# Thirty-two tokens of a 384-token dense stage move to a gathering stage that packs four slots into a step

## The chip, the core and the metric

One core of a Trainium2 chip runs the whole program. The metric is the device time of one execution in microseconds, and the time of a kernel is the median of several executions. The core has five engines that run side by side, each in its own program order: TensorE (PE, with its weight loads as PEld), VectorE (DVE), ScalarE (ACT), GpSimd (POOL) and SyncE (SP). SP does nothing but issue DMAs; ACT and POOL issue some too. Semaphores order one engine behind another.

## The reference, cut to what matters

The reference is two layers of an encoder trunk on 512 tokens (two sequences of 256) of width 1024. Each layer has a token mixer and a PEER channel mixer. Only PEER is touched:

```python
q = (ht @ wq).reshape(T, 8, 256)                       # 8 heads
s1, s2 = q[..., :128] @ k1.T, q[..., 128:] @ k2.T      # 128 keys each
v1, i1 = top_k(s1, 16); v2, i2 = top_k(s2, 16)
vs, ic = top_k(v1[..., :, None] + v2[..., None, :], 16)    # of 256 pairs
idx = i1[ic // 16] * 128 + i2[ic % 16]                 # an expert of 16384
g = softmax(vs)
a = einsum('td,thkd->thk', x, u_tab[idx])              # 8*16 = 128 slots a token
y = einsum('thk,thkd->td', g * gelu(a), v_tab[idx])
```

So every token picks 128 of 16384 experts; an expert is one row of 1024 in `u_tab` and one in `v_tab`.

## The kernel before, in words

All 512 tokens lie in columns, channels in partitions. `hH` and `hL` hold the normed input as a high and a low part in fp32r, and each product with a weight is made of three matmuls (`mm3`, L181 to L184): high weight by low data, high by high, low weight by high data. Weights come two chunks of 128 at a time as one 1 MB load (`wraw`, L133), are cast to the high part by ACT (`wh`, L120), and DVE (in the stages u and v) or POOL (elsewhere) subtracts to get the low part (`wl`, L121). Two buffers of each exist.

PEER of a layer runs in this order. **Queries** (`queries`, L737): 16 products of 512 columns, then scores against the keys (L744) and, on DVE, the sixteen largest of each (`top16`, L730). Early in it `row_copy` (L411) turns the last 128 tokens by PE and ACT into `hrow`, one token to a partition. **Routing** (`route`, L778) finds experts and weights of 128 tokens at a time on DVE.

Then the tokens go two ways. The first 384 (`TD`) are **dense**. Stage u (the loop over c, 128 chunks) multiplies all of `u_tab` by them: 24 matmuls of 384 columns a chunk, then GELU on ACT (L1011, L1017), and most results go to HBM (`a_d`). Between these, `gates` (L862) builds the tokens' gate matrices from one-hots: for four tokens two DVE instructions (L894, L898) and eight small matmuls (L872), and ACT's copy goes to HBM (`g_d`). Stage v (the loop over n, 128 chunks) reads both back (`va`, `vg`), multiplies them (`wf`, L995), splits (`sH`, `sL`) and multiplies with all of `v_tab`, again 24 matmuls of 384 columns a chunk, summed in eight PSUM banks.

The last 128 tokens are **gathered** (`gathered`, L911), token to partition. Step j of 128 fetches the 128 rows of `u_tab` that slot j of each token names (an indirect DMA of 128 rows by 4 KB issued by POOL, L926, four buffers, three ahead) and DVE multiplies and sums them with `hrow` (L937). After that 128 steps fetch rows of `v_tab`, and DVE adds each, weighted, to `yrow` (L945). At the end PE turns `yrow` back (L1082), and `residual` (L541) adds all of it to x.

The order on each engine is written out by hand. In stage u, `gathered` advances by at most 1.1 steps a chunk for 64 chunks, then so that `GU` steps are done by chunk 127; `gates` advances at 0.9 four-token steps a chunk until chunk 64 and then evenly until chunk 101; `route_tiles` (L839) routes the three dense tiles of 128 meanwhile. In stage v the rest of the steps are spread over 124 chunks. `tc.issue_after(st["last"])` puts these instructions behind the latest weight subtraction on DVE.

```python
while done - 1 < (GS * (c - c0) if c < CM else
                  GS * (CM - c0) + (GU - GS * (CM - c0)) * (c - CM) / (127 - CM)):
```

`norm` (L383) writes `hH`, `hL`, and with L404 a copy `hq` of the last 128 tokens.

## Time and profile before

| what | value |
|---|---|
| median of 3 runs | 3411.75 us (3403.14 to 3413.47) |
| the profiled execution's own time | 3406.75 us |
| its span, first to last instruction | 3404.9 us |
| mean granted TensorE clock | 0.978 |
| stage u of layer 0 | 618.9 to 1212 us |
| stage v of layer 0 with the residual | 1212 to 1750 us |
| stage v of layer 1 with the residual | 2863.4 to 3401 us |

A row of a profile names line, engine, operation and tiles as out<-in. Busy time of PE is the time in which at least one matmul is under way; since matmuls overlap, the distance between starts tells its pace. The DMA share is the time that packets took, over 16 engines and the stretch; it goes over 1 where packets of two queues overlap. A wait is named by who waited and for whom.

### The profile page before, as it was taken

Reading aid. Unit: us, or ns where it says so; the run is one execution under the profiler, and the core shown is the slowest. Engines: PE = TensorE matmul, PEld = TensorE weight load, DVE = VectorE, ACT = ScalarE, POOL = GpSimd, SP = SyncE. Lnnn points to the kernel's source line nnn. Section 1 sums busy time; section 2 is a strip of 40 time slices with the busy share of each in tenths; the row PEclk is TensorE's granted clock in tenths of the full one; section 3 lists DMA queues with packets and bytes.
Section 4 is the critical chain, followed back from the end, with each engine's and each line's share of the span. In section 5 each row is a group of like instructions: output and inputs, shape, how many; then the busy total and the mean of one; then the engine's idle time right before and its main releaser. Section 6 shows DMA issues by size and latency. Waiting matters only on the chain.

```text
span 3404.9 us, 47985 instructions
## 1 busy us (share of the span) xinstructions
PE 3274.4 (96%) x18758; PEld 3034.7 (89%) x18758; DVE 2714.8 (80%) x4689; ACT 1346.2 (40%) x1631; POOL 1106.9 (33%) x682
## 2 busy tenths in 40 slices
PE   7999979999999999999989998899999999999999
PEld 3778758999999999999978886689999999999999
DVE  6797997998898567777766589899979866777776
ACT  3443223345566333333335432334546543333232
POOL 4322453143232322333333234314423233223331
PEclk9999989999999999999989998899999999999999
DMA  6332552389899989999932236317999997899996
GB/s 244 123 137 88 197 193 88 138 313 351 314 349 344 317 287 321 348 339 356 341 131 86 87 137 214 119 72 278 340 335 331 345 340 280 302 351 335 348 334 238
DMA packets 271414, 867.46 MB, mean 255 GB/s; under 512 B 20241, under 2 KB 119633, under 8 KB 222801
## 3 DMA queue, kind: packets, MB, share of 16 engines
q1 hardware_dynamic: 174418, 500.49, 41.9%
q0 software_dynamic: 73728, 268.47, 22.0%
q10 hardware_dynamic: 23040, 95.43, 7.2%
q8 instruction: 147, 2.41, 0.3%
q14 instruction: 81, 0.66, 0.1%
HBM read 764.17 MB, written 97.52 MB: 253 GB/s over the span
## 4 chain that ended last, share of the span: by engine, by line
PE 72%; DVE 16%; DMA 7%; issue 3%; ACT 1%; POOL 1%; SPq 0%; DVEq 0%; ACTq 0%; POOLq 0%
PE y L182 9%; PE y L184 9%; PE y L183 9%; PE a L182 9%; PE a L184 9%; PE a L183 9%; DVE junk L259 5%; DMA wraw<-w_st 3%; PE G L872 3%; PE zin L182 2%; PE zin L183 2%; PE zin L184 2%; DMA mraw<-w_modT 2%; DVE wl L121 1%; PE q L182 1%
## 5 line engine op out<-in xcount | busy, mean ns | idle before, releaser
L120 ACT CAST wh<-wraw 128x2048 fp32r<-128x2048 f32 (+1 forms) x380 | 610.0, 1611 | 1185.8 <-PE y L183 354.2
L121 DVE TENSOR_TENSOR wl<-wraw,wh 128x2048 fp32r<-128x2048 f32 x248 | 568.3, 2291 | 371.3 <-ACT wh L120 371.0
L182 PE MATMUL a<-hL,wh 128*128 128x384 f32 x2048 | 698.8, 341 | 0.4 <-ACT wh L120 0.2
L184 PE MATMUL a<-hH,wl 128*128 128x384 f32 x2048 | 688.5, 336 | 10.9 <-DVE wl L121 10.9
L182 PE MATMUL y<-sL,wh 128*128 128x384 f32 x2048 | 686.2, 335 | 2.0 <-DVE sL L121 1.9
L183 PE MATMUL a<-hH,wh 128*128 128x384 f32 x2048 | 686.8, 335 | 0.0
L184 PE MATMUL y<-sH,wl 128*128 128x384 f32 x2048 | 684.5, 334 | 0.0
L183 PE MATMUL y<-sH,wh 128*128 128x384 f32 x2048 | 684.4, 334 | 0.0
L926 POOL DMA_INDIRECT row<-u_rows,idx x256 | 359.0, 1402 | 806.7 <-DVE row L937 563.8
L926 POOL DMA_INDIRECT row<-v_rows,idx x256 | 338.0, 1320 | 733.1 <-DVE yrow L945 698.5
L121 POOL TENSOR_TENSOR wl<-wraw,wh 128x1024 fp32r<-128x1024 f32 x132 | 359.3, 2741 | 645.3 <-ACT wh L120 645.3
L184 PEld LDWEIGHTS a<-hH,wl 128*128 128x128 f32 x2048 | 385.7, 188 | 14.0 <-DVE wl L121 14.0
L182 PEld LDWEIGHTS y<-sL,wh 128*128 128x128 f32 x2048 | 384.5, 188 | 4.2 <-DVE sL L121 3.7
L182 PEld LDWEIGHTS a<-hL,wh 128*128 128x128 f32 x2048 | 385.7, 188 | 1.0 <-ACT wh L120 1.0
L183 PEld LDWEIGHTS a<-hH,wh 128*128 128x128 f32 x2048 | 385.9, 188 | 0.0
L183 PEld LDWEIGHTS y<-sH,wh 128*128 128x128 f32 x2048 | 384.6, 188 | 0.0
L184 PEld LDWEIGHTS y<-sH,wl 128*128 128x128 f32 x2048 | 384.5, 188 | 0.0
L945 DVE SCALAR_TENSOR_TENSOR yrow<-row,ga,yrow 128x1024 f32<-128x1024 f32 x254 | 325.3, 1281 | 0.2
L259 DVE SCALAR_TENSOR_TENSOR junk<-mraw,cb 128x1024 bf16<-128x1024 f32 x176 | 304.6, 1731 | 21.4 <-DMA mraw<-w_modT 17.7
L937 DVE SCALAR_TENSOR_TENSOR row<-row,hrow 128x1024 f32<-128x1024 f32 x256 | 308.7, 1222 | 4.5 <-DMA row<-u_rows,idx 4.5
L182 PE MATMUL zin<-hL,wh 128*128 128x512 f32 x544 | 219.8, 404 | 4.9 <-DVE hL L406 4.8
L184 PE MATMUL zin<-hH,wl 128*128 128x512 f32 x544 | 215.5, 396 | 1.7 <-POOL wl L121 1.7
(255 smaller groups left out, 4616.7 us busy)
## 6 DMA issues: line engine op xcount, KB each, us to landing
wraw<-w_st SPq DMA_DIRECT2D x314, 1024.0 KB
g_d<-stg ACTq DMA_DIRECT2D x48, 1024.0 KB
vg<-g_d SPq DMA_DIRECT2D x32, 1536.0 KB
mraw<-w_modT SPq DMA_DIRECT2D x88, 512.0 KB
a_d<-a ACTq DMA_DIRECT2D x104, 384.0 KB
va<-a_d SPq DMA_DIRECT2D x52, 768.0 KB
pre<-w_st SPq DMA_DIRECT2D x8, 1024.0 KB
wsh<-w_mod SPq DMA_DIRECT2D x8, 512.0 KB
```

What stands on the lines that cost most here:

```text
L120: nc.scalar.copy(h, src)
L121: return (engine or nc.vector).tensor_sub(lo, src, h.bitcast(F32))
L182: nc.tensor.matmul(out, lhsT=a[0], rhs=b[1], start=first, stop=False)
L183: nc.tensor.matmul(out, lhsT=a[0], rhs=b[0], start=False, stop=False)
L184: st["pe"] = nc.tensor.matmul(out, lhsT=a[1], rhs=b[0], start=False, stop=last).ins
L259: st["mod"] = nc.vector.scalar_tensor_tensor(junk, w, 1.0, cb[:, s, :], op0=OP.mult, op1=OP.mult, accum_out=modc[l][:, j, s:s + 1]).ins
L872: nc.tensor.matmul(p[:, k, :], lhsT=oh[:, k // 2, 1, :, k % 2], rhs=o1[:, k // 2, n, :, k % 2], start=n == 0, stop=n == 1)
L926: nc.gpsimd.indirect_dma_start(out=r[:, :], out_offset=None, in_=tab[:, :], in_offset=bass.IndirectOffsetOnAxis(ap=idx[:, j:j + 1], axis=0))
L937: nc.vector.scalar_tensor_tensor(r, r, 1.0, hrow, op0=OP.mult, op1=OP.mult, accum_out=a[:, j:j + 1])
L945: nc.vector.scalar_tensor_tensor(yrow, r, a[:, j:j + 1], yrow, op0=OP.mult, op1=OP.add)
```

## The change

`TD` falls from 384 to 352: the dense stages and `gates` handle 32 tokens less. Those tokens, numbers 352 to 383, join the gathering. 32 more steps for each table serve them: the 128 partitions of a step hold 32 tokens four times, and partition group g takes the slots 32g to 32g+31, so a token's 128 slots are done in 32 steps. Their routing is still made with the third tile; four DMAs on SP's queue copy it into `egx` in that layout. `hqx` is a copy of these tokens in the norm, POOL repeats it four times along the columns, and PE and ACT turn it into a second `hrow`. The second `yrow` holds four partial sums per token, and one fp32 matmul per 128 channels with a 0/1 matrix `fold_x` adds them up at the end. It takes over the buffer of `hq`. `GU` rises from 132 to 178, out of 320 steps (`STEPS`) in place of 256.

```diff
...
@@ -34,13 +34,16 @@
 T = 512
 TS = 256
 NT = 4
-TD = 384
+NX = 32
+XG = 128 // NX
+TD = 384 - NX
 ND = TD // 16
 VG = 8
 NC = 64
 CAND = ((0, 0, 1, 16), (16, 1, 4, 8), (40, 4, 8, 4), (56, 8, 16, 1))
 GSCALE = 32768.0
-GU = 132
+GU = 178
+STEPS = 256 + 2 * NX
 R0 = 104
 GEND = 101
 PRE = 4
...
@@ -401,19 +404,29 @@
                 for c, B, A in half:
                     st["act"] = nc.scalar.activation(hH[:, k, c], t1[:, c], AF.Identity, bias=B).ins
                 if hq is not None:
-                    nc.scalar.activation(hq[:, k, :], t1[:, TD:], AF.Identity, bias=half[1][1])
+                    nc.scalar.activation(hq[:, k, :], t1[:, 384:], AF.Identity, bias=half[1][1])
+                    nc.scalar.activation(hqx[:, k, :], t1[:, TD:384], AF.Identity, bias=half[1][1])
                 for c, B, A in half:
                     st["dve"] = nc.vector.scalar_tensor_tensor(hL[:, k, c], t1[:, c], B, hH[:, k, c].bitcast(F32),
                                                                op0=OP.add, op1=OP.subtract).ins
                 filler = pull(filler, 2)
             run_all(filler or [])
 
-    def row_copy(hrow, hq):
-        for q in range(2):
-            p = bank([128, 4, 128], "hn")
-            for k in range(4):
-                nc.tensor.transpose(p[:, k, :], hq[:, 4 * q + k, :], ident)
-            nc.scalar.copy(hrow[:, q * 512:(q + 1) * 512], p.rearrange("p a b -> p (a b)"))
+    def row_copy(pool_, hrows, hq, hqx):
+
+        for i, hrow in enumerate(hrows):
+            for q in range(2):
+                p = bank([128, 4, 128], "hn")
+                for k in range(0, 4, 2):
+                    src = hq[:, 4 * q + k:4 * q + k + 2]
+                    if i:
+                        h = hqx[:, 4 * q + k:4 * q + k + 2]
+                        src = pool_.tile([128, 2, 128], F32, name="hx")
+                        nc.gpsimd.tensor_copy(src.rearrange("p k (g t) -> p k g t", t=NX),
+                                              h[:, :, None].to_broadcast([128, 2, XG, NX]))
+                    for c in range(2):
+                        nc.tensor.transpose(p[:, k + c, :], src[:, c, :], ident)
+                nc.scalar.copy(hrow[:, q * 512:(q + 1) * 512], p.rearrange("p a b -> p (a b)"))
 
 
     def mixer(l, fx):
...
@@ -836,12 +849,17 @@
         nc.vector.tensor_mul(eg[:, 2], eg[:, 2], z[:, :, None].to_broadcast([128, H, TOPK]))
         yield 1.0
 
-    def route_tiles(l, rp, pools, iotak, val, ixu, tiles):
-        for t in range(TD // 128):
+    def route_tiles(l, rp, pools, iotak, val, ixu, tiles, egx):
+        for t in range(3):
             while len(tiles) > 1:
                 yield 1.0
             eg = rp.tile([128, 3, NH, TOPK], F32, name="eg", bufs=1)
             yield from route(rp, iotak, val, ixu, t, eg)
+            if t == 2:
+                ef = eg.rearrange("p j h k -> p j (h k)")
+                for g in range(XG):
+                    nc.sync.dma_start(egx[g * NX:(g + 1) * NX], ef[128 - NX:, :, g * NX:(g + 1) * NX])
+                st["egx"] = l
             for _ in range(EGD):
                 yield 10.0
             p = bank([128, 3, 128], "egT")
@@ -879,12 +897,12 @@
             if g == 3:
                 nc.scalar.dma_start(g_d[l][t * 8 + b], stg.pop(b))
 
-        for tt in range(TD // 128):
+        for tt in range(3):
             while not tiles:
                 yield 1
             t, E16, g16 = tiles[0]
             rp = pools[0]
-            for b in range(8):
+            for b in range(min(8, ND - 8 * t)):
                 for g in range(4):
                     t0 = b * 16 + g * 4
                     oh = rp.tile([128, 2, 2, 128, 2], F16, name="o12", bufs=LAG + 2)
@@ -908,20 +926,29 @@
                 yield 1
             tiles.pop(0)
 
-    def gathered(l, gp, rp, iotak, val, ixu, eg, hrow, yrow):
+    def gathered(l, gp, rp, iotak, val, ixu, eg, egx, hrows, yrows):
+
+
         yield from route(rp, iotak, val, ixu, NT - 1, eg, HS, NH)
         yield ROUTED
         ef = eg.rearrange("p j h k -> p j (h k)")
-        idx = gp.tile([128, 128], U32, name="idx")
-        nc.vector.tensor_scalar(ef[:, 0], ef[:, 0], 128.0, float(l * 16384), op0=OP.mult, op1=OP.add)
-        nc.vector.tensor_add(idx, ef[:, 0], ef[:, 1])
-        a = gp.tile([128, 128], F32, name="ga")
+        idx = gp.tile([128, 128 + NX], U32, name="idx")
+        a = gp.tile([128, 128 + NX], F32, name="ga")
+
+        def index(e, c):
+            nc.vector.tensor_scalar(e[:, 0], e[:, 0], 128.0, float(l * 16384), op0=OP.mult, op1=OP.add)
+            nc.vector.tensor_add(idx[:, c], e[:, 0], e[:, 1])
+
+        index(ef, slice(0, 128))
         rows = {}
-        seq = [(tab, j) for tab in (u_rows, v_rows) for j in range(128)]
+        seq = [(tab, j) for tab in (u_rows, v_rows) for j in range(128 + NX)]
         AHEAD = 3
 
         def fetch(i):
             tab, j = seq[i]
+            if tab is u_rows and j == 128:
+                assert st["egx"] == l
+                index(egx, slice(128, 128 + NX))
             r = gp.tile([128, D], F32, name="row", bufs=AHEAD + 1)
             nc.gpsimd.indirect_dma_start(out=r[:, :], out_offset=None, in_=tab[:, :],
                                          in_offset=bass.IndirectOffsetOnAxis(ap=idx[:, j:j + 1], axis=0))
@@ -933,22 +960,25 @@
             if i + AHEAD < len(seq):
                 fetch(i + AHEAD)
             r = rows.pop(i)
-            if i < 128:
+            hrow, yrow, n = (hrows[1], yrows[1], NX) if j >= 128 else (hrows[0], yrows[0], 32)
+            if tab is u_rows:
                 nc.vector.scalar_tensor_tensor(r, r, 1.0, hrow, op0=OP.mult, op1=OP.mult, accum_out=a[:, j:j + 1])
-                if j % 32 == 31:
-                    c = slice(j - 31, j + 1)
+                if j % n == n - 1:
+                    c = slice(j - n + 1, j + 1)
                     nc.scalar.activation(a[:, c], a[:, c], AF.Gelu)
-                    nc.vector.tensor_mul(a[:, c], a[:, c], ef[:, 2, c])
-            elif j == 0:
-                nc.vector.tensor_scalar(yrow, r, a[:, 0:1], None, op0=OP.mult)
+                    w = egx[:, 2, :] if j >= 128 else ef[:, 2, c]
+                    nc.vector.tensor_mul(a[:, c], a[:, c], w)
+            elif j % 128 == 0:
+                nc.vector.tensor_scalar(yrow, r, a[:, j:j + 1], None, op0=OP.mult)
             else:
                 nc.vector.scalar_tensor_tensor(yrow, r, a[:, j:j + 1], yrow, op0=OP.mult, op1=OP.add)
             yield 1.15
 
-    def peer(l, hrow, hq):
+    def peer(l, hrows, hq, hqx):
         with ExitStack() as px:
             gp = px.enter_context(pool(name=f"gp{l}", bufs=1))
-            yrow = gp.tile([128, D], F32, name="yrow")
+            yrows = [gp.tile([128, D], F32, name="yrow"), hq.rearrange("p k n -> p (k n)")]
+            egx = gp.tile([128, 3, NX], F32, name="egx")
             iotak = gp.tile([128, TOPK, TOPK], F16, name="iotak")
             iota = gp.tile([128, 128], F32, name="iota")
             nc.sync.dma_start(iota, c_iota)
@@ -962,14 +992,14 @@
             prx = ExitStack()
             rb = prx.enter_context(pool(name=f"pr{l}", bufs=1, side=RIGHT))
             eg = gp.tile([128, 3, NH, TOPK], F32, name="egl")
-            queries(l, val, ixu, hrow, hq, rb, route(rp, iotak, val, ixu, NT - 1, eg, 0, HS))
+            queries(l, val, ixu, hrows, hq, hqx, rb, route(rp, iotak, val, ixu, NT - 1, eg, 0, HS))
             vx = ExitStack()
             vp = None
             gx = ExitStack()
             pools = []
-            ga = gathered(l, gp, rp, iotak, val, ixu, eg, hrow, yrow)
+            ga = gathered(l, gp, rp, iotak, val, ixu, eg, egx, hrows, yrows)
             tiles = []
-            rt = route_tiles(l, rp, pools, iotak, val, ixu, tiles)
+            rt = route_tiles(l, rp, pools, iotak, val, ixu, tiles, egx)
             gt = gates(l, pools, iota2, tiles)
             res = {}
             ablk, gblk = {}, {}
@@ -1031,7 +1061,7 @@
                             gq = 1
                         g0 = SG * (min(c + 1, CG) - c1)
                         with tc.issue_after(st["last"]) if B2 else ExitStack():
-                          while gt is not None and gq - 1 < g0 + (104 - g0) * max(0, c + 1 - CG) / (GEND - CG):
+                          while gt is not None and gq - 1 < g0 + (4 * ND + 8 - g0) * max(0, c + 1 - CG) / (GEND - CG):
                             gt = pull(gt, 1)
                             gq += 1
                     with tc.issue_after(st["last"]):
@@ -1070,7 +1100,7 @@
                             ds_ = slice(d * 128, (d + 1) * 128)
                             mm3(y[d][:, :TD], (w[0][:, ds_], w[1][:, ds_]), s, n == 0, False)
                     with tc.issue_after(st["last"]):
-                        while done - 1 < min(256, GU + (256 - GU) * (n + 1) / 124):
+                        while done - 1 < min(STEPS, GU + (STEPS - GU) * (n + 1) / 124):
                             next(ga)
                             done += 1
                     if n == 126:
@@ -1079,7 +1109,8 @@
                     ds_ = slice(d * 128, (d + 1) * 128)
                     for w, s, last in tail:
                         mm3(y[d][:, :TD], (w[0][:, ds_], w[1][:, ds_]), s, False, last)
-                    nc.tensor.transpose(y[d][:, TD:], yrow[:, ds_], ident)
+                    nc.tensor.transpose(y[d][:, 384:], yrows[0][:, ds_], ident)
+                    nc.tensor.matmul(y[d][:, TD:384], lhsT=yrows[1][:, ds_], rhs=fold_x, start=True, stop=True)
                     residual(l, 40, d, y[d], 0, T)
 
 
...
```

The part left out adds `fold_x` to the constants, and hands the new tiles through `queries` and `peer`.

## Rows read from the trace of the kernel before

**Rows 1.** The page's first part: busy time, share of the span and instructions of each engine.
```profile
PE 3274.4 (96%) x18758; PEld 3034.7 (89%) x18758; DVE 2714.8 (80%) x4689; ACT 1346.2 (40%) x1631; POOL 1106.9 (33%) x682
```
**Rows 2.** The chain that ended last, from 618 to 1750 us, by line.
```profile
by line: PE y L184 15.5%; PE y L182 15.5%; PE y L183 15.5%; PE a L182 13.7%; PE a L184 13.5%; PE a L183 13.4%; PE G L872 4.0%; DMA wraw<-w_st 1.5%; DVE wl L121 1.4%; DMA row<-u_rows,idx 1.1%; POOL acc L359 0.7%; issue 0.5%; DVE scr L732 0.4
```
**Rows 3.** The timeline of PE: start, duration; 256 columns, then 384, 18 intervals each.
```profile
253.79 0.28 PE L182 MATMUL iv<-idft,y 128*128 128x256 f32 x1
...
255.94 0.28 PE L182 MATMUL iv<-idft,y 128*128 128x256 f32 x1
...
2999.82 0.33 PE L183 MATMUL y<-sH,wh 128*128 128x384 f32 x1
...
3002.94 0.33 PE L183 MATMUL y<-sH,wh 128*128 128x384 f32 x1
```
**Rows 4.** Stretches: length, each engine's busy us, PEclk, DMA share, GB/s.
```profile
533.00:618.00 85.00, 83.60 (x427) 71.12 (x425) 77.63 (x487) 31.75 (x48) 27.30 (x12) 1.00 0.25 88
618.90:769.00 150.10, 146.49 (x887) 143.28 (x885) 147.03 (x451) 68.82 (x80) 55.14 (x34) 0.99 0.70 249
769.00:916.00 147.00, 147.00 (x973) 143.19 (x971) 121.49 (x226) 72.64 (x81) 45.66 (x36) 1.00 0.92 333
916.00:1076.00 160.00, 160.00 (x1185) 155.08 (x1184) 146.06 (x206) 99.16 (x106) 45.24 (x34) 1.00 0.93 345
1076.00:1212.00 136.00, 134.05 (x818) 132.63 (x816) 82.48 (x93) 52.94 (x59) 43.64 (x33) 1.00 0.88 313
1212.00:1750.00 538.00, 533.85 (x3082) 533.32 (x3081) 406.14 (x326) 174.09 (x137) 167.44 (x129) 1.00 0.92 322
1500.00:1520.00 20.00, 20.00 (x118) 20.00 (x117) 14.73 (x13) 5.42 (x5) 5.10 (x5) 1.00 1.07 375
2863.40:3401.00 537.60, 535.28 (x3081) 532.98 (x3080) 405.51 (x325) 166.93 (x126) 159.24 (x121) 1.00 0.90 318
```
**Rows 5.** DVE's groups, 916 to 1076 us: count, busy us, mean ns, idle before.
```profile
L937 DVE SCALAR_TENSOR_TENSOR row<-row,hrow 128x1024 f32<-128x1024 f32 x35 | 42.6, 1223 | 0.0
L121 DVE TENSOR_TENSOR wl<-wraw,wh 128x2048 fp32r<-128x2048 f32 x17 | 38.9, 2290 | 3.0 <-ACT wh L120 3.0
L898 DVE TENSOR_TENSOR o<-o,g 128x1024 f16<-128x1024 f16 x51 | 34.6, 692 | 11.0 <-PE G L872 11.0
L894 DVE TENSOR_TENSOR o<-E,iota 128x1024 f16<-128x1024 f16 x51 | 33.6, 690 | 0.0
```
**Rows 6.** DVE's groups, 1212 to 1750 us.
```profile
L945 DVE SCALAR_TENSOR_TENSOR yrow<-row,ga,yrow 128x1024 f32<-128x1024 f32 x124 | 158.8, 1281 | 0.0
L121 DVE TENSOR_TENSOR wl<-wraw,wh 128x2048 fp32r<-128x2048 f32 x63 | 144.4, 2292 | 123.3 <-ACT wh L120 123.2
```
**Rows 7.** DMA view, 1212 to 1750 us: rate in 40 slices, packets, two issue lines.
```profile
GB/s 239 333 288 280 354 237 342 356 289 371 315 333 401 303 371 294 357 392 315 370 307 357 401 286 369 323 344 399 309 372 316 360 370 318 378 302 328 213 163 111
DMA packets 73961, 173.04 MB, mean 322 GB/s; under 512 B 3648, under 2 KB 46656, under 8 KB 65856
...
vg<-g_d SPq DMA_DIRECT2D x14, 1536.0 KB
va<-a_d SPq DMA_DIRECT2D x24, 768.0 KB
```
**Rows 8.** DMA view, 916 to 1076 us: rate in 40 slices, packets.
```profile
GB/s 415 258 225 326 390 374 360 374 122 276 406 374 268 426 414 373 421 395 287 410 369 372 338 306 327 316 347 312 249 416 428 375 378 365 328 356 322 329 344 334
DMA packets 11571, 55.21 MB, mean 345 GB/s; under 512 B 1292, under 2 KB 1292, under 8 KB 7846
```
**Rows 9.** The tile row, whole span: the gathers on POOL, and their landing.
```profile
L926 POOL DMA_INDIRECT row<-v_rows,idx x256: 933/1408/3616, 1184.4 to 3367.1; - x128
...
DMA to landing us min/median/max: 4.9/8.1/10.4
```
**Rows 10.** The timeline around the row copy of layer 0: start, duration.
```profile
531.74 4.73 POOL L121 TENSOR_TENSOR wl<-wraw,wh 128x1024 fp32r<-128x1024 f32 x2 [33.42 <-ACT wh L120]
...
532.16 1.04 PE L415 MATMUL hn<-mats,hq 128*128 128x128 f32 x8
...
533.62 0.49 DVE L731 MAX8 val<-sc 128x8 f32<-128x128 f32 x2 [14.59 <-ACT sc L747]
```
**Rows 11.** ACT's groups, 500 to 519 us (the norm ahead of PEER).
```profile
L404 ACT ACTIVATE hq<-t,modc 128x128 f32<-128x128 f32 x8 | 3.1, 391 | 0.0
```
**Rows 12.** PE's groups, 3390 to 3403 us (the end of layer 1).
```profile
L1082 PE MATMUL y<-mats,yrow 128*128 128x128 f32 x8 | 2.2, 271 | 0.0
```

19 lines of the change are left out of this document (10 added, 9 removed).

## The prediction

> **What bounds the kernel now.** I read the page first: PE is busy for 96% of the span and DVE for 80% [rows 1], so PE leads, but an average hides the stages. The chain that ended last tells where. From 618 to 1750 us, stages u and v of layer 0, the matmuls of u and v hold 87% of it and the gate matmuls 4% [rows 2]. So the matmuls' own pace sets these stages, and the next view must give it: with 384 columns 18 starts take 3.12 us, 173.3 ns each, with 256 columns 2.15 us, 119.4 ns each [rows 3]. That is 0.421 ns a column. The stretches show what stands next in line [rows 4]. Stage u falls into four of about 32 chunks each. DVE is busy for 147.0 of 150.1 us in the first, 121.5 of 147 in the second, 146.1 of 160 in the third, 82.5 of 136 in the fourth. In stage v it has 406 of 538 us. The DMA share is 0.88 to 0.93 everywhere after the first stretch. Two other resources are thus near their limits, and a shorter matmul pays only where neither is reached first.
>
> **The shorter matmuls.** At 352 columns the line between the two paces gives 173.3 - 32 x 0.421 = 159.8 ns, 13.5 ns less. A stage has 128 x 24 = 3072 such matmuls, so PE's need falls by 41.4 us in each of the four stages (166 us in all), or 10.4 us in a quarter of stage u. The weight loads do not hold the pace, because 119 ns was reached with one for every matmul [rows 3].
>
> **The gathering's extra work in stage u.** Up to chunk 64 nothing moves: 1.1 steps a chunk. Behind it come 46 more steps than before (178 for 132) over 63 chunks, 23.4 in each of the last two quarters. Each costs DVE 1.22 us [rows 5] and the DMA engines 128 rows of 4 KB, 0.524 MB. Eight of 96 gate steps fall away; some seven of them lie in the third quarter, each with 0.69 + 0.69 us of DVE [rows 5] and 1.05 MB / 4 of stores.
>
> First quarter: DVE is already busy for 147.0 of 150.1 us and its work is unchanged. PE can gain 3 us at most; I take 1. Second quarter: PE 147.0 - 10.4 = 136.6, DVE 121.5, so all 10 us arrive. Third quarter: DVE needs 146.1 + 23.4 x 1.22 - 7 x 1.38 = 165 us, PE at most 150, and the bytes become 55.2 [rows 8] + 12.3 - 2.3 = 65.2 MB. Slices of 4 us reached 428 GB/s there, the mean was 345 [rows 8]: 152 to 189 us. I take 400 GB/s, since slices of 13 us in stage v reached 401 [rows 7] and 20 us held 375 [rows 4]; that makes 163 us, under DVE's 165. With a little for the two meeting: 167, a loss of 7. Fourth quarter: DVE 82.5 + 28.5 = 111, PE 134 - 10.4 = 124, bytes 0.313 x 136 = 42.6 + 12.3 - 0.7 = 54.2 MB, at 400 GB/s 136 us. PE's gain is lost to the transfers; with some unevenness 139, a loss of 3. **Stage u: 1 + 10 - 7 - 3, a gain of 1 us** out of 593 (between 21, rival a, and -21, rival b).
>
> **Stage v.** 142 steps for 124, so 18 more at 1.28 us [rows 6] or 23 us of DVE, which then has at most 429 us of work for 497, and covers it: the time in which it waited for ACT's cast before a weight subtraction, 123 us [rows 6], takes the new steps. Bytes: 173.0 + 9.4 - 3.4 (a twelfth of 14 vg and 24 va loads) = 179.0 MB [rows 7]. PE alone would end the stage after 538 - 41 = 497 us. By rate over share, 322 / 0.92 = 350 GB/s, the transfers take 511 us; at 375 GB/s [rows 4] 477. I take 503: **a gain of 35 us a layer** (25 to 41). What is late next is a weight load or a row behind another queue's packets.
>
> **Smaller parts, per layer.** Row copy: PE must turn the repeated tokens, and its transposes stand in program order behind four POOL copies through one buffer. The nearest row is POOL's subtraction of 1024 columns, 4.73 / 2 = 2.4 us [rows 10]; a quarter of that is 0.6, two transposes are 0.26 (1.04 / 8 each [rows 10]), four rounds 3.4 us. POOL is also busy until 536.5 with two subtractions, while PE would be there at 533.2: 3.3 us more. Behind the waiting transposes stand the scores, and DVE waits for those. But DVE has just started its first scores at 533.6 [rows 10] and is the fuller engine behind (77.6 of 85 us, then 147 of 150 [rows 4]), so PE's 7 us come back in part; I take 3 (0 to 8). Two more ACT copies lie beside it. Norm: eight ACT instructions, each under the 391 ns of four times the columns [rows 11], 0 to 3 us; taken 0.5, because PE still has the queries to do. SP's queue: four DMAs, 49 KB together, wait there for DVE's routing of the third tile, with weight loads behind; but those wait for later DVE work in any case, so nothing, and if DVE ran behind by a routing instruction about 1 us. POOL's further 64 gathers at 1.4 us [rows 9] lie in its idle time. Fold: eight fp32 matmuls of 32 columns in the closing chain, each under the 271 ns of the transposes there [rows 12]: taken 1.5 us (0 to 2.2). **Together 5 us lost** (1 to 13).
>
> **Sum.** 1 + 35 - 5 = 31 us a layer, 62 us in two. The profiled execution took 3406.75 us (span 3404.9 and 1.85 around it), so 3344.75. It is 5.0 us under the median of the three runs, 3411.75; on that median the forecast is **3350 us**, or -1.8%.
>
> **The rivals.**
> (a) PE stays the bound almost everywhere: DVE's surplus in the third quarter is taken up by its idle time in the second and fourth. For it: DVE has 54 us idle in the fourth. Against it: instructions are issued in a fixed order, so idle time cannot be borrowed back. With the third quarter level and the fourth 10 us shorter stage u gains 21, v 41, the small parts take 3: 59 a layer, 3411.75 - 118 = 3294.
> (b) The DMA engines have no more to give than rate over share tells: 345 / 0.93 = 371 GB/s in the third quarter makes 176 us (+16), 313 / 0.88 = 356 in the fourth 152 us (+16), and v takes 511 (-27). With -1 and -10 of the first quarters and 5 of the small parts that is -1 a layer, 3410. For it: shares of 0.9. Against it: the share counts packets twice where two queues overlap, and 1.07 at 375 GB/s is such a stretch [rows 4]. The Trainium skill, in "DMA: Bandwidth & Descriptors", section "Where 436 GB/s comes from", says that the memory side binds transfers from HBM at about 358 GB/s for a core; by that the third quarter would take 182 us, the fourth 151, stage v 500, and the whole about 3400. The trace does not agree with it as a ceiling: 401 GB/s stood over 13 us [rows 7].
> (c) Slower: the loop of four row buffers binds. A buffer is free again after landing (8.1 us median, 10.4 at most [rows 9]) and one DVE step of 1.22 us. The fourth quarter asks for 57 steps in 136 us, 2.39 us each, which the loop gives up to a landing of 4 x 2.39 - 1.2 = 8.3 us: that is the point. At 10.4 us a step takes 2.9 us, so 165 us (+29). DVE takes its instructions in order, so weight subtractions stand behind late rows in the third quarter too: 58 steps with half a microsecond of waiting on half of them add some 14 on top of the 7 (+21). Stage v gains only 25. Per layer -1 - 10 + 21 + 29 - 25 + 5 = +19, 3450. For it: landings lengthen with the load. Against it: before, the loop was never the last wait in u or v but 1.1% of the chain [rows 2].
> (d) The change does not do what it says, because the pace does not follow the columns: the stages stay and the small parts come on top, 3422. Only the two paces of [rows 3] speak to it, and 352 lies between them.
>
> **How the numbers follow.** Forecast 0.50, (a) 0.18, (b) 0.18, (c) 0.12, (d) 0.02. A difference under 0.3%, about 10 us, cannot be told from no change. Faster: forecast, (a) and a third of (b) that keeps a little more, 0.75. Within 0.3%: the middle of (b), 0.09. Slower: (c), (d) and the lower end of (b), 0.16. The range must leave out 2 in 10 at most: from (a), 3290, to a little above (b), 3415, which leaves (c), (d) and tails beyond the ends.
>
> **What would show it.** Starts of u and v matmuls 160 ns apart, and gaps between them with ACT's cast or DVE's subtraction as releaser, in the second half of stage u above all. DVE busy for over 97% in the third quarter, with no idle time for G; DMA over 380 GB/s in the fourth quarter and in v. Stage u of about 590 us, stage v of about 503. A wait of PE for POOL's `hx` of 5 to 8 us in all. The prediction is wrong if stage u shortens by over 20 us or lengthens by over 20, or if stage v shows the 41 us in full, or half of it.

## The result, and the profile after

The changed kernel takes 3496.07 us (median of four runs, 3493.85 to 3503.44) against 3410.7 us, a ratio of 1.026 (95%: 1.0245 to 1.0275): **slower by 2.6%**, where 1.8% faster was forecast, and outside the range. The profiled execution took 3503.44 us (span 3501.6, mean granted clock 0.953 for 0.978 before).

The page's rows of PE and DVE (compare [rows 1]), and the two rows of the gathering's steps:
```profile
PE 3187.6 (91%) x18678; PEld 2933.5 (84%) x18678; DVE 2833.2 (81%) x4855; ACT 1320.8 (38%) x1637; POOL 1412.5 (40%) x818
...
L965 DVE SCALAR_TENSOR_TENSOR row<-row,hrow 128x1024 f32<-128x1024 f32 x320 | 387.0, 1220 | 132.7 <-DMA row<-u_rows,idx 131.8
L974 DVE SCALAR_TENSOR_TENSOR yrow<-row,ga,yrow 128x1024 f32<-128x1024 f32 x254 | 325.3, 1281 | 42.3 <-DMA row<-v_rows,idx 40.2
```
PE is busy for 87 us less, not the 166 by which its need was to fall, and stands idle for 314 us instead of 130. DVE now waits 132 us for rows of `u_rows`; in the kernel before it waited 4.5 us over the whole span, and 0.0 in the part of stage u shown in [rows 5].

Stretches, with the columns of [rows 4]: the queries, stage u in four, u whole and v of layer 0, then u and v of layer 1.
```profile
516.50:629.20 112.70, 107.33 (x531) 90.50 (x529) 83.01 (x504) 40.97 (x66) 29.68 (x15) 0.97 0.20 75
629.20:780.00 150.80, 138.31 (x873) 135.51 (x873) 143.30 (x442) 64.44 (x76) 53.49 (x33) 0.94 0.67 237
780.00:923.00 143.00, 142.55 (x1013) 138.97 (x1012) 126.71 (x236) 74.62 (x83) 46.26 (x37) 1.00 0.95 354
923.00:1090.00 167.00, 144.39 (x1020) 138.02 (x1019) 145.10 (x212) 85.67 (x94) 83.88 (x50) 0.93 0.92 338
1090.00:1267.60 177.60, 144.24 (x888) 140.31 (x887) 120.63 (x146) 56.46 (x64) 91.14 (x60) 0.93 0.92 333
629.20:1267.60 638.40, 569.49 (x3788) 552.81 (x3788) 535.74 (x1033) 281.20 (x316) 274.77 (x179) 0.95 0.87 316
1267.60:1801.00 533.40, 505.85 (x3097) 502.38 (x3096) 424.87 (x347) 168.14 (x133) 228.71 (x147) 0.97 0.94 340
2334.00:2961.00 627.00, 569.62 (x3789) 551.95 (x3788) 536.72 (x1033) 280.82 (x317) 273.18 (x179) 0.95 0.88 322
2961.00:3498.50 537.50, 504.65 (x3097) 501.03 (x3095) 424.56 (x348) 163.72 (x126) 229.83 (x142) 0.97 0.92 333
```
Per layer, on the mean of the two, the queries took 7.5 us more, stage u 40 us more, and stage v was no shorter. That is 93 of the 97 us between the two profiled executions. The matmuls themselves did what was forecast: 27 intervals of 352 columns take 4.30 us, 159.3 ns each (timeline of PE: start, duration).
```profile
1699.69 0.32 PE L186 MATMUL y<-sH,wh 128*128 128x352 f32 x1
...
1703.99 0.32 PE L186 MATMUL y<-sH,wh 128*128 128x352 f32 x1
```
In the second half of stage u the waits tell who is late (923 to 1267 us: who waited for whom, then us in total, how often, and the longest):
```profile
POOL row L953 <- DVE row L965: 123.2, 57, 6.5
DVE row L965 <- DMA row<-u_rows,idx: 65.1, 28, 6.6
PEld a L187 <- DVE wl L124: 59.7, 19, 6.6
...
ACT wh L123 <- DMA wraw<-w_st: 30.9, 8, 6.7
```
Read them as a ring. POOL waits for a DVE step to free a row buffer, DVE waits for the row, and PE waits for a weight subtraction that stands behind that step on DVE. One turn of it in the timeline (start, duration, and in brackets the idle time before):
```profile
1096.43 2.75 POOL L953 DMA_INDIRECT row<-u_rows,idx  x1 [3.44 <-DVE row L965]
...
1108.43 1.23 DVE L965 SCALAR_TENSOR_TENSOR row<-row,hrow 128x1024 f32<-128x1024 f32 x1 [3.02 <-DMA row<-u_rows,idx]
...
1109.59 2.29 DVE L124 TENSOR_TENSOR wl<-wraw,wh 128x2048 fp32r<-128x2048 f32 x1
...
1111.93 0.66 PE L187 MATMUL a<-hH,wl 128*128 128x352 f32 x1 [4.02 <-DVE wl L124]
```
The row asked for at 1096.43 is the fourth step later on DVE. It lands 12 us after its issue began, and DVE had stood for 3.0 us. PE then stood for 4.0 us until the subtraction behind it was done.

### The profile page after: what moved, and what is told of

The parts are those of the page before. It is cut to its first block, busy times and chain, and to the rows that moved or that the text cites. A ratio compares the mean times of both kernels' runs of the same rounds, so it can differ in the third digit from the quotient of the medians.

```text
span 3501.6 us, 48333 instructions
## 1 busy us (share of the span) xinstructions
PE 3187.6 (91%) x18678; PEld 2933.5 (84%) x18678; DVE 2833.2 (81%) x4855; ACT 1320.8 (38%) x1637; POOL 1412.5 (40%) x818
## 4 chain that ended last, share of the span: by engine, by line
PE 34%; DVE 22%; DMA 17%; issue 15%; POOL 9%; ACT 2%; POOLq 0%; SPq 0%; DVEq 0%; ACTq 0%
POOL row L953 8%; DMA wraw<-w_st 7%; DMA row<-v_rows,idx 5%; DVE junk L262 5%; PE y L185 4%; PE y L186 4%; PE y L187 4%; DMA row<-u_rows,idx 3%; DVE wl L124 3%; PE a L187 3%; PE a L185 3%; PE a L186 3%; PE zin L185 2%; PE zin L186 2%; PE zin L187 2%
## 5 line engine op out<-in xcount | busy, mean ns | idle before, releaser
L187 PE MATMUL a<-hH,wl 128*128 128x352 f32 x2048 | 685.8, 336 | 121.4 <-DVE wl L124 121.0
L953 POOL DMA_INDIRECT row<-u_rows,idx x320 | 488.1, 1525 | 720.6 <-DVE row L965 427.3
L953 POOL DMA_INDIRECT row<-v_rows,idx x320 | 512.5, 1601 | 597.1 <-DVE yrow L974 425.4
L185 PE MATMUL y<-sL,wh 128*128 128x352 f32 x2048 | 671.9, 328 | 57.0 <-DVE sL L124 57.0
L185 PE MATMUL a<-hL,wh 128*128 128x352 f32 x2048 | 693.0, 338 | 2.7 <-ACT wh L123 2.7
L186 PE MATMUL a<-hH,wh 128*128 128x352 f32 x2048 | 679.5, 332 | 0.0
L187 PE MATMUL y<-sH,wl 128*128 128x352 f32 x2048 | 666.6, 325 | 2.4 <-DVE wl L124 2.4
L186 PE MATMUL y<-sH,wh 128*128 128x352 f32 x2048 | 667.2, 326 | 0.0
L187 PEld LDWEIGHTS a<-hH,wl 128*128 128x128 f32 x2048 | 401.7, 196 | 136.2 <-DVE wl L124 136.0
L965 DVE SCALAR_TENSOR_TENSOR row<-row,hrow 128x1024 f32<-128x1024 f32 x320 | 387.0, 1220 | 132.7 <-DMA row<-u_rows,idx 131.8
```

The lines of the kernel that those rows point to most:

```text
L185: nc.tensor.matmul(out, lhsT=a[0], rhs=b[1], start=first, stop=False)
L186: nc.tensor.matmul(out, lhsT=a[0], rhs=b[0], start=False, stop=False)
L187: st["pe"] = nc.tensor.matmul(out, lhsT=a[1], rhs=b[0], start=False, stop=last).ins
L953: nc.gpsimd.indirect_dma_start(out=r[:, :], out_offset=None, in_=tab[:, :], in_offset=bass.IndirectOffsetOnAxis(ap=idx[:, j:j + 1], axis=0))
L965: nc.vector.scalar_tensor_tensor(r, r, 1.0, hrow, op0=OP.mult, op1=OP.mult, accum_out=a[:, j:j + 1])
```

## The experiments

The first theory was the ring of row buffers in stage u and the rate of the transfers in stage v. The rivals were DVE's work, the bytes in u as well, PE's fallen clock, the queries' copies and, from run 16 on, a ring of weight buffers in v. Stages are measured from their first matmul to the first of the next stage, v to the end of the residual; layer 0 / layer 1, in us, from one profiled execution of each kernel. Each ratio is against the kernel before on the same chip. In the diffs `...` stands for lines left out.

| kernel | median us | ratio (95%) | queries | u | v |
|---|---|---|---|---|---|
| before | 3410.7 | | 104.4/105.6 | 593.1/592.9 | 534.6/538.2 |
| after | 3496.07 | 1.026 (1.0245-1.0275) | 112.7/112.2 | 638.4/626.9 | 534.2/537.7 |
| 1 dense part alone | 3331.71 | 0.9765 (0.9737-0.9793) | 111.5/114.3 | 567.6/564.8 | 518.5/515.8 |
| 2 gathering alone | 3540.51 | 1.0377 (1.0347-1.0407) | 104.4/106.4 | 644.7/643.1 | 550.8/555.6 |
| 3 half the bytes | 3336.44 | 0.9779 (0.9732-0.9826) | 111.6/112.8 | 595.4/590.7 | 492.7/494.2 |
| 4 half DVE's steps | 3431.16 | 1.006 (1.0037-1.0082) | 112.7/112.9 | 605.9/610.5 | 530.1/529.6 |
| 5 GU 132 | 3464.94 | 1.0163 (1.0143-1.0183) | 112.7/112.7 | 568.6/570.1 | 585.4/581.0 |
| 6 early copies | 3488.57 | 1.0233 (1.0213-1.0253) | 105.5/107.6 | 631.9/627.3 | 537.5/542.9 |
| 7 = 6, 5 buffers | 3419.88 | 1.002 (1.0001-1.004) | 105.5/108.0 | 598.6/601.2 | 533.5/536.0 |
| 8 16 tokens | 3412.39 | 1.0014 (1.0003-1.0024) | 112.7/113.4 | 589.4/591.4 | 537.5/531.9 |
| 9 = 7, 16 tokens | 3397.7 | 0.9972 (0.9958-0.9986) | 105.5/107.6 | 587.9/586.1 | 538.6/537.0 |
| 10 = 7, 6 buffers | 3407.55 | 1.0011 (0.9996-1.0027) | 105.5/106.8 | 594.6/595.2 | 529.4/530.6 |
| 11 before, 5 buffers | 3412.25 | 1.0024 (1.0013-1.0036) | 104.4/107.0 | 591.3/592.0 | 535.9/537.8 |
| 12 filler matmuls | 3510.96 | 1.0312 (1.029-1.0334) | 111.2/113.3 | 641.9/645.6 | 533.0/529.4 |
| 13 = 10, half DVE | 3349.81 | 0.9823 (0.9799-0.9847) | 105.5/107.6 | 577.5/578.1 | 525.4/528.0 |
| 14 = 10, half bytes | 3293.28 | 0.9657 (0.9636-0.9679) | 105.5/107.4 | 577.2/578.1 | 492.7/492.9 |
| 15 = 6, 16 tokens | 3405.14 | 0.9981 (0.9969-0.9992) | 105.5/106.7 | 586.2/584.6 | 541.8/544.7 |
| 16 third weight buffer in v | 3415.15 | 1.0018 (1.0008-1.0028) | 112.8/113.9 | 627.6/630.7 | 498.2/497.9 |
| 17 = 10 and 16 | 3332.26 | 0.9767 (0.975-0.9785) | 105.5/107.7 | 600.1/601.5 | 492.9/492.9 |
| 18 = 9 and 16 | 3355.01 | 0.9843 (0.983-0.9857) | 105.5/106.7 | 587.0/587.2 | 516.6/516.6 |

**1. The dense part alone**: matmuls of 352 columns and `hx` as changed, but the old 256 steps.
```diff
-GU = 178
-STEPS = 256 + 2 * NX
+GU = 132
+STEPS = 256
...
-        seq = [(tab, j) for tab in (u_rows, v_rows) for j in range(128 + NX)]
+        seq = [(tab, j) for tab in (u_rows, v_rows) for j in range(128)]
```


> The changed kernel without the 64 extra gather steps of a layer (so the 32 tokens get no result), GU back at 132; the matmuls of u and v keep 352 columns. It tells what the shorter matmuls are worth alone. Theory T (transfers: the extra rows overload the DMA engines, and PE waits for weights and rows): with the old number of rows PE sets stage v again, about 497 us for 534, and stage u comes to 560 to 570 us for 593; the whole about 3290 us. Theory D (DVE's added work is what delays PE): the same 497 in v, stage u about 570, 3300 us. Theory R (the loop of four row buffers is too slow): the same, 3290. If the pace did not follow the columns: about 3425.

Measured: 80 us less than before, where PE's need fell by 166. Stage v is the surprise (columns of [rows 4]):
```profile
1197.90:1716.40 518.50, 499.17 (x3098) 496.28 (x3096) 397.42 (x326) 168.05 (x133) 174.16 (x127) 0.99 0.92 328
```
Without one added step it stops at 518, though its matmuls need 492 (run 3), and PE is idle for 19 us. All three theories put on record had 497. Something that the old columns hid holds the stage already.

**2. The gathering alone**: 64 more steps a layer, with the dense part as before (`TD = 384`; the new steps repeat slots, and `fold_x` is left out).
```diff
-GU = 132
+GU = 178
+NX = 32
+STEPS = 256 + 2 * NX
...
-        seq = [(tab, j) for tab in (u_rows, v_rows) for j in range(128)]
+        seq = [(tab, j) for tab in (u_rows, v_rows) for j in range(128 + NX)]
...
```


> The kernel before with 64 extra gather steps a layer (the first 32 slots once more, into sums that nothing uses) at the change's schedule (GU 178 of 320), dense matmuls of 384 columns, no row copy, no fold. It tells what the extra steps cost alone. T: the second half of stage u moves 97.8 + 24.6 = 122 MB at the 336 GB/s that the changed kernel had there, 364 us for 296, and stage v some 10 us more: about 3560. R: 57 steps a quarter at about 3.0 us make 171 and 171 us for 160 and 136, stage v unchanged: about 3505. D: the third quarter 175 us for 160, nothing else: about 3440. If the steps cost nothing while PE is slower: 3411.

Measured: +129 us, 51 in each stage u and 17 in each stage v. Steps and dense part do not add: -80 and +129 make 49, and the whole change costs 85.

**3 and 4. Half of each row.** Run 3 fetches 2 KB of each row, and DVE multiplies the other half of the buffer too, which was filled with zeros at the start; run 4 fetches all and lets DVE read half of it. So half of the gathered sums is left out of the computation.
```diff
...
-            nc.gpsimd.indirect_dma_start(out=r[:, :], out_offset=None, in_=tab[:, :],
+            nc.gpsimd.indirect_dma_start(out=r[:, 0:512], out_offset=None, in_=tab.rearrange("n (h d) -> (n h) d", h=2),
```
```diff
-                nc.vector.scalar_tensor_tensor(r, r, 1.0, hrow, ...)
+                nc.vector.scalar_tensor_tensor(r[:, 0:512], r[:, 0:512], 1.0, hrow[:, 0:512], ...)
...
```


> The changed kernel, each gather step fetches only the first half of every row (2 KB for 4 KB), DVE's work stays whole (the other half is zero, so the result of the gathered tokens is partial). T: the gathered bytes halve, PE sets stage v again (about 497 us) and stage u falls to some 575: about 3320. R: the landing shortens too, less than by half, so stage u about 590 and v 500 to 520: 3360 to 3400. D: unchanged, about 3490.

> The changed kernel, each gather step fetches the whole row, but DVE multiplies and adds only the first 512 of 1024 columns (partial result of the gathered tokens). D: DVE's steps cost 0.6 us less, the third quarter is no longer bound by it and stage u falls to 575: 3320 to 3400. T: the bytes stay, about 3480. R: a step of the loop is 0.6 / 4 = 0.15 us shorter, 0.15 x 114 = 17 us a layer: about 3460.

Measured, stage v of run 3 and then of run 4:
```profile
1221.00:1713.70 492.70, 491.75 (x3097) 491.48 (x3096) 424.33 (x348) 167.25 (x133) 206.00 (x148) 1.00 0.84 292
```
```profile
1229.50:1759.50 530.00, 504.73 (x3097) 500.82 (x3096) 349.74 (x348) 168.08 (x133) 192.57 (x148) 0.98 0.94 343
```
With half the bytes PE is busy for 491.75 of 492.70 us at full clock: v is then PE's alone, and the 41 us are there. With 75 us less of DVE, v keeps 530. So DVE does not hold v, and the bytes do, by their rate or by how long one load takes; the two are told apart in run 16. Stage u falls in both, by 36 to 43 us and by 16 to 33, which does not tell bytes and DVE from the ring, since both make a turn of it shorter.

**5. The steps at the old pace in stage u**: 46 of them move to v.
```diff
-GU = 178
+GU = 132
```


> The changed kernel with GU 132 for 178: the 46 added steps of stage u move to stage v, which then does 188. T: stage u falls to the 566 us that it has without the added steps, stage v moves some 205 MB at 340 GB/s, 600 us for 534; the whole about 3490, no better. D (DVE's steps delay PE): stage u 566 too, stage v has 484 us of DVE work, so stays near 534; about 3360. R: a step every 3.2 us gives 188 x 3.2 = 600 us, as T; this run does not part T from R.

Measured: u falls to 569, 24 us under before, and v rises by 51 us in layer 0, at 348 GB/s. Most of the loss moves with the steps; the whole is 3465.

**6. The copies ahead of their use.** POOL makes `hx` in one go at the start of the queries, into the buffer of `yrow`, and not in between the transposes.
```diff
+            hx = yrows[0].rearrange("p (k n) -> p k n", k=KD)
...
+            for k in range(0, KD, 2):
+                nc.gpsimd.tensor_copy(hx[:, k:k + 2].rearrange("p k (g t) -> p k g t", t=NX),
+                                      hqx[:, k:k + 2, None].to_broadcast([128, 2, XG, NX]))
...
```


> The changed kernel with POOL's four repeating copies moved to the start of the queries, where POOL is idle, into a tile of their own (the buffer of yrow), so that PE's transposes find them done. If PE's wait for POOL is what lengthened the queries from 105 to 112 us, they fall back to 105, and the first quarter of stage u with its long weight waits shortens too: 3470 to 3480. If that time would have been lost to DVE's top-16 work anyway: 3490 or more.

Measured: the queries take 105.5 and 107.6 us, 7.2 and 4.6 less, so the copies' place cost them that. Of the whole, 7.5 us come back; in the profiled execution v takes some 4 us a layer more.

**7. A fifth row buffer**, on top of 6, in room won by laying `iota` over `yrow` and `hqx` over the second `hrow`.
```diff
-        AHEAD = 3
+        AHEAD = 4
...
-            iota = gp.tile([128, 128], F32, name="iota")
+            iota = yrows[0][:, 0:128]
...
-            hqx = hrp.tile([128, KD, NX], F32, name="hqx")
+            hqx = hrows[1][:, 0:KD * NX].rearrange("p (k n) -> p k n", k=KD)
```


> As e6, with five row buffers for four (fetching four ahead); two small tiles share other buffers to make room. R: a step of the loop takes four fifths of the time, 2.4 for 3.0 us, the late half of stage u falls by some 50 us a layer and the whole to about 3380. T: the bytes stay and so does the time, within 15 us of e6. D: as T.

Measured: 3419.88, so 69 us under run 6 from one buffer of 512 KB. Stage u falls from 631.9 and 627.3 to 598.6 and 601.2, 30 us a layer; v by 5. DVE's row:
```profile
L965 DVE SCALAR_TENSOR_TENSOR row<-row,hrow 128x1024 f32<-128x1024 f32 x320 | 385.6, 1218 | 66.8 <-DMA row<-u_rows,idx 66.6
```
Its waits for rows are half of the 131.8 us above. The gathers of the second half of u tell the pace: count, duration min/median/max, first and last start. Of the kernel before (from 916 us), of after (from 923), and of run 7 (from 923), each to the end of u:
```profile
L926 POOL DMA_INDIRECT row<-u_rows,idx x59: 933/1146/2937, 921.7 to 1178.0; - x59
```
```profile
L953 POOL DMA_INDIRECT row<-u_rows,idx x91: 935/1442/3052, 923.0 to 1214.8; - x91
```
```profile
L953 POOL DMA_INDIRECT row<-u_rows,idx x88: 932/1550/3052, 922.5 to 1173.7; - x88
```
That is a step every 4.4 us before (256.3 / 58), every 3.24 us after (291.8 / 90) and every 2.89 us with five buffers (251.2 / 87). The forecast asked for 2.4 to 2.9.

**8 and 9. Sixteen tokens** in place of 32, with eight slots of each in a step: 32 steps a layer more and matmuls of 368 columns; run 8 is the change with that, run 9 is run 7 with that.
```diff
-NX = 32
+NX = 16
...
-GU = 178
+GU = 155
```
Run 9 also keeps 16 chunks of GELU results on chip and not 24, for room (`R0 = 112`).

> The changed kernel with half the tokens moved: NX 16, so 368 dense tokens, 16 more steps a table with eight slots each, GU 155. If loss and gain grow evenly: halfway, about 3453. T says that the cost begins only where the transfers are full, and they were nearly so before: 3420 to 3440. If the four-buffer loop is the limit and has some slack left up to about 1.4 steps a chunk: 3390 to 3410, better than before.

> Half the tokens (NX 16, GU 155) as in e8, with the early copies of e6 and the five row buffers of e7; to make room 112 instead of 104 chunks of stage u's results go through HBM (1.5 MB more each way a layer). R: stage u, 590 us in e8, loses the row loop's part and falls to 570 to 575, the queries lose 7, stage v stays at about 533: 3365 to 3380, better than both kernels. If transfers hold stage u as well: 3395 to 3415.

Measured: run 8 is 0.14% over before, no difference that can be told. Run 9, at 3397.7 and a ratio of 0.9972, is 0.28% under before, at the edge of what can be told. All of its gain is in u (6 us a layer).

**10. A sixth buffer** on top of 7 (`AHEAD = 5`, `R0 = 112`, one score tile less), **and 11, the control**: five buffers in the kernel before, `yrow` laid over `hq`.
```diff
-        AHEAD = 4
+        AHEAD = 5
...
-                s = qp.tile([128, NT, 128], F32, name="sc", bufs=3)
+                s = qp.tile([128, NT, 128], F32, name="sc", bufs=2)
```
```diff
-        AHEAD = 3
+        AHEAD = 4
...
-            yrow = gp.tile([128, D], F32, name="yrow")
+            yrow = hq.rearrange("p k n -> p (k n)")
```


> As e7 (32 tokens, GU 178), with six row buffers for five, and 112 chunks through HBM and two score buffers for three to make room. R: stage u falls once more, from 600 to 580 or less, the whole to about 3385. If the transfers are the next limit of stage u: 600 us again or a little more for the added bytes, the whole 3415 to 3435.

> The kernel before with five row buffers for four (yrow shares the buffer of hq to make room). There a landed row waited some 8 us for DVE, so the loop had room: 3410, within 0.3% of before. If it falls by 30 us or more, the gain of e7 does not belong to the change.

Measured: the sixth gives u another 5 us (594.6 and 595.2), the level of before; DVE's wait for rows of u falls to 44.5 us. In the kernel before a fifth buffer gives 1 to 2 us in u and nothing in the whole (a ratio of 1.0024). So the ring did not bind before, and **the change made it bind**.

**12. Filler.** Eight matmuls by a zero weight in each chunk from 64 on, ahead of those that wait for `wl`, to keep PE busy where it waited.
```diff
+                    for _ in range(8):
+                        nc.tensor.matmul(p, lhsT=zero, rhs=hH[:, 0, :TD], start=False, stop=False)
...
```


> The changed kernel, with eight matmuls of zero weights (which add nothing to the result) in each of chunks 64 to 127 of stage u, put right ahead of the matmul at which PE waits for DVE's weight subtraction, about 1.3 us a chunk. Theory K (the fall of TensorE's clock behind these waits, which took 30 us of stage u, costs time of its own): the clock stays up and stage u falls from 633 to about 610, the whole to 3450. If the clock only fills time in which PE would have waited: stage u within 10 us of 633, the whole 3490 to 3515. If the added matmuls are on the path: up to 41 + 41 us more, 3580.

Measured, the third and fourth stretch of u:
```profile
925.00:1090.00 165.00, 165.00 (x1216) 161.72 (x1215) 146.14 (x213) 82.12 (x90) 70.47 (x52) 1.00 0.93 345
1090.00:1268.00 178.00, 178.00 (x1160) 176.96 (x1160) 121.32 (x141) 57.22 (x64) 79.43 (x60) 1.00 0.91 331
```
The granted clock is at its full level (2.4 GHz) in both, and stage u is no shorter for it: 641.9 and 645.6 us, 3.5 and 19 more than after. That is what 82 us of filler (512 matmuls of 159 ns) cost, so most of it fell into time in which PE waited. It is PE work itself, though, so by itself the run does not say what the clock cost.

**13 and 14. Half of DVE's steps and half of the bytes again**, now with six buffers (the edits of runs 4 and 3 on run 10, and the same parts left out).

> As e10 (six row buffers), DVE multiplies and adds only the first 512 columns of each gathered row (partial result of the gathered tokens). It tells what holds stage u, 595 us, once the row loop is wide. D: DVE's steps set the pace behind the loop, stage u falls by 25 us or more, to 570. T: transfers do, stage u stays within 8 us of 595. Stage v: within 5 us of 530 by T.

> As e10, each step fetches 2 KB of each row for 4 KB, DVE's work whole. T: stage u falls by 15 us or more below 595, stage v to 493. D: stage u stays within 8 us of 595 (e3 with four buffers had 593), stage v falls to 493 all the same.

Measured, stage u of run 13, then of run 14:
```profile
619.10:1196.60 577.50, 551.60 (x3787) 539.10 (x3787) 451.26 (x1036) 280.66 (x316) 219.98 (x183) 0.97 0.93 355
```
```profile
621.70:1198.90 577.20, 553.45 (x3788) 538.01 (x3788) 538.77 (x1036) 281.55 (x316) 282.92 (x182) 0.98 0.78 274
```
With the ring eased, DVE's work and the bytes are worth the same 17 us each in stage u. For run 13 that lies between what the theories had on record (25 or more, or at most 8). By quarters of 32 chunks, on the mean of the layers, half of DVE's steps is worth 8, 2, 8 and 0 us, and half of the bytes 1, 0, 5 and 10. In v run 14 has 492.7 us again, and run 13 525.4.

**15. Sixteen tokens with early copies alone**: four buffers, `GU = 140`.
```diff
-NX = 32
+NX = 16
...
-GU = 178
+GU = 140
```


> Sixteen tokens moved, the early copies of e6, four row buffers, 104 chunks through HBM as in the change, GU 140 for 155. From e8 (3412): the queries give back 7 us a layer, and 15 steps fewer in stage u of the 1 us or so that each cost there, against some 0.7 us each in stage v: 3385 to 3395, 0.5% better than the kernel before. If stage v takes what stage u gives: 3398, as e9.

Measured: 3405.14, 0.19% under before, which is no difference that can be told.

**16. A third buffer for raw weights, in stage v alone.** The chain of after in v, 1267.6 to 1801 us, had led there. Its pieces in order of time (start, length, what):
```profile
1585.91 16.11 DMA wraw<-w_st
1602.12 1.91 ACT wh L123
...
1620.84 16.26 DMA wraw<-w_st
```
Five such pieces stand some 35 us apart from 1585.91 to 1723.50. SP's timeline shows why: each is the load that SP issues right behind a `va` of 704 KB and a `vg` of 1408 KB on the same queue.
```profile
1581.19 0.33 SPq L1010 DMA_DIRECT2D va<-a_d  x1
1581.57 0.48 SPq L1014 DMA_DIRECT2D vg<-g_d  x1
1585.91 8.11 SPq L136 DMA_DIRECT2D wraw<-w_st  x2
```
With two buffers a load, its cast (1.9 us) and its subtraction (2.29 us, [rows 6]) must be done within four chunks of matmuls: 96 x 159.3 ns = 15.3 us, and 16.6 at 384 columns. `extra` is the pool of stage v while v runs; 16 chunks of GELU results stay on chip and not 24, for the room.
```diff
+            x = st.get("extra")
+            if x and j % 3 == 2 and 2 * j < st["limit"]:
+                raw[j] = x.tile([128, 2, 1024], F32, name="wx", bufs=1)
...
-        while st["load"] < min(len(order) // 2, j + 2):
+        while st["load"] < min(len(order) // 2, j + 2 + (st.get("extra") is not None and 2 * j + 4 < st["limit"])):
...
```


> The change with a third buffer for raw weights in stage v alone (16 chunks of GELU results kept on chip for the room, not 24). If stage v is held by a ring of weight buffers (two of 1 MB; a load took 14.6 to 16.7 us in the chain of v, and cast and subtraction take 1.9 and 2.3 us before the buffer is free, against 2 x 7.65 us of matmuls), v falls from 534 to 500 to 512 a layer, with DMA over 355 GB/s, and the whole by 45 to 70 us, to about 3440. If it is held by the rate that its mix of transfers reaches, 340 to 348 GB/s, v stays within 525 to 538 and the waits for weights turn into waits for rows. Stage u is untouched: 627 to 640.

Measured: 3415.15, 81 us under after. Stage v takes 498.2 and 497.9, stage u is as it was. The stretch of v, layer 0, and the wait for weights in it:
```profile
1252.00:1750.20 498.20, 493.67 (x3098) 493.11 (x3096) 429.05 (x349) 167.20 (x133) 207.95 (x148) 1.00 0.98 366
```
```profile
ACT wh L123 <- DMA wraw<-w_st: 3.5, 1, 3.5
```
Much the same bytes (182.4 MB for 181.2) now move at 366 GB/s, and the casts wait 3.5 us for weights, not 125.9. **A ring of weight buffers held stage v**, not a rate. The clock stands at 1.00 with nothing done to it: its fall to 0.97 in v came from the waits.

**17 and 18. The rings opened together**: the third weight buffer, with the edit of run 16, on run 10 and on run 9. For the room run 17 keeps 8 chunks of GELU results on chip.
```diff
-R0 = 112
+R0 = 120
```

> Run 10 (six row buffers, early copies) with the third weight buffer in v, and 8 chunks of GELU results kept on chip. Weight ring: v falls from 530 to 495 to 507, u stays at 595, the whole at 3335 to 3365, under the kernel before. Rate of the mix: v 525 to 535 and 3400 to 3415. u is untouched by either.

> Run 9 (16 tokens, five row buffers, early copies) with the third weight buffer in v. PE needs 128 x 24 x 166.5 ns = 512 us there. Weight ring: v falls from 538 to 515 to 522, the whole to 3355 to 3370. Rate of the mix: v 532 to 540 and 3390 to 3400.

Measured: 3332.26, a ratio of 0.9767 (0.975 to 0.9785), **2.3% under the kernel before and 164 us under the change as it was made**; with 16 tokens 3355.01 (0.9843). Stage v of run 17:
```profile
1219.30:1712.20 492.90, 491.94 (x3097) 491.67 (x3095) 423.40 (x346) 167.16 (x133) 199.06 (x145) 1.00 0.99 371
```
PE is busy for 491.94 of 492.90 us with every byte fetched, so v is PE's alone. Stage u stands at 600 and 601.5, 8 over before.

## Why the prediction was wrong

**The sum.** The forecast had per layer 1 us gained in u, 35 in v and 5 lost. Measured: 40 lost in u, 0 gained in v, 7.5 lost in the queries. The sum weighed each engine's work and the bytes, and it was near right for a kernel that is held by these: with both rings opened and the copies moved (run 17) the gain is 77 us, where 62 were forecast. That nearness is in part luck: v gained 44 us a layer for 35, and u lost 8 where 1 was to be gained. **What failed is that two rings of buffers, each too short for the new pace, had no term in it.**

**Stage u: the step that failed is the one that set rival (c) aside.** The forecast gave the last two stretches 167 and 139 us. They took 167.0 and 177.6, and the third held fewer chunks (PE's groups of the third, then the fourth stretch; eight of these matmuls make a chunk):
```profile
L187 PE MATMUL a<-hH,wl 128*128 128x352 f32 x232 | 80.4, 347 | 20.9 <-DVE wl L124 20.8
```
```profile
L187 PE MATMUL a<-hH,wl 128*128 128x352 f32 x267 | 91.0, 341 | 33.4 <-DVE wl L124 33.4
```
That is 5.76 us a chunk (167 / 29) for 5.2 forecast, and 5.32 for 4.3. Of the signs that the prediction named, DVE busy for over 97% of the third quarter and over 380 GB/s in the fourth did not come either: DVE had 145.10 of 167 us, and 333 GB/s were moved. The prediction put the point of rival (c) at a landing of 8.3 us, beside a measured median of 8.1 [rows 9], and still gave it 0.12, on the ground that the loop had been only 1.1% of the chain before. But before, a step came every 4.4 us; what bears on the change is the landing against the new pace. In the tile row of run 6, which has the same four buffers:
```profile
DMA to landing us min/median/max: 4.4/8.4/13.6
```
The median hardly moved. The longest is 13.6 for 10.4, but the trace before marks the landing of one gather in eight and that of run 6 of every one. By the rival's own formula a landing of 8.4 allows a step every 2.4 us, and 3.24 was measured. What it left out stands in the trace of run 6, in the second half of stage u of layer 0. On the mean a free buffer waited 0.7 us for POOL's issue, the row landed 8.8 us after the issue began, waited 1.8 us until DVE came to it, and was used for 1.2: 12.6 us a turn, or 3.1 us a step with four buffers. Before, the seven landings marked in that part were followed by a wait of 8.6 us for DVE, and that was the room which the ring had. Runs 7, 10 and 11 show the size: 30 us a layer for the fifth buffer, 5 for the sixth, none before the change. With six u stands at 595, 2 us over before, where the sum had 1 us of gain. In it DVE and the bytes share the third quarter and the bytes hold the fourth (runs 13, 14), as the sum had them. The second stretch gave its 10 us (4.28 us a chunk for 4.59 before); the first gave none.

**Stage v: the step that failed is "what is late next is a weight load", named and costed at nothing.** The forecast of 503 us lay between PE's 497 and 511 at 350 GB/s. (It started from 538 us for layer 0; up to the end of the residual, as in the table, that stage took 534.6.) After the change the stage took 534, and 498 once a third weight buffer was there (run 16), so work and rate were sized well. The waits of v before its change were in the trace that the prediction read: 1.5% of the chain [rows 2]. In the list of waits of the kernel before, 1212 to 1750 us, and then of after, 1267.6 to 1801:
```profile
ACT wh L120 <- DMA wraw<-w_st: 75.3, 10, 7.8
```
```profile
ACT wh L123 <- DMA wraw<-w_st: 125.9, 20, 11.9
```
Ten late loads cost PE little while four chunks lasted 16.6 us: it was busy for 533.6 of the 534.5 us to the end of the residual in layer 0, and for 535.28 of 537.60 in layer 1 [rows 4]. At 15.3 us they reach it, with the added gathers on the same engines. Run 1, with the old steps, shows the first alone (518 for 492). Runs 3 and 14 took the bytes away and so made loads short; read alone they speak for a limit of the rate as well, which run 16 refutes.

**The rivals.** (b), the rate over share, fell: with the ring opened v moves 371 GB/s at a share of 0.99 (run 17), so 340 at 0.94 was not all that there was. The Trainium skill, in "DMA: Bandwidth & Descriptors", section "Where 436 GB/s comes from", gives about 358 GB/s as what the memory side lets a core have. The trace does not agree with it as a ceiling, as the prediction said: run 17 moved 371 GB/s over 493 us. (c) was right in its mechanism and its sign, and its price for stage u was right too. It had -1, -10, +21 and +29 us for the four quarters; counted from the first matmul of chunks 0, 32, 64 and 96, on the mean of the layers, they changed by +3, -10, +17 and +29. Its 38 us in all were under the 85 measured, since it let v gain 25. (a) is what v became with the ring opened. (d) fell with the pace: 159.3 ns for 159.8 forecast.

**The small parts.** The queries lost 7.5 us, not 3: the bound of 8 was the measured case, and DVE's idle time did not take PE's wait back. Run 6 gives 7.2 and 4.6 of it back. The first wait of the transposes for POOL, forecast as 3.3 us, measured 3.39, and all such waits came to 4.0 us a layer where 5 to 8 were forecast:
```profile
538.80 0.69 PE L428 MATMUL hn<-mats,hx 128*128 128x128 f32 x2 [3.39 <-POOL hx L425]
```
The sum lacked what came behind it: from 538.8 to 545.2 us the granted clock was 0.50, the 1.2 GHz level, and matmuls of the queries started 0.43 us apart, for 0.23 once it was back at 1.00. That DVE has room in v was right (run 4).

**Open:** the 8 us by which u of run 17 stands over before. In the last quarter alone it is 15 over (155 us on the mean of the layers for 140), and the second gives 9 back. Run 10 took 148 us for the last quarter; run 17 sends eight more chunks of GELU results to HBM there, but that these cost the 7 us between the two is not shown. What the fallen clock cost by itself in stage u is not shown either (run 12). A third weight buffer in stage u was not tried, nor one in v of the kernel before, where PE was idle for 1 us in layer 0 and 2 to 3 in layer 1 and so had no more than that to win.
